# Two rows of output-norm gates: summed over partitions by square turns and memory instead of products with ones

## The chip, the cores and the metric

The kernel runs on one core of one Trainium2 chip. The metric is the device time of one execution in microseconds (us). Three runs of the kernel before took 1633.28, 1633.6 and 1634.9 us; their median, 1633.6 us, is the time that the prediction starts from. Engines are called TensorE (PE, and PEld for its weight loads), VectorE (DVE), ScalarE (ACT), GpSimd (POOL) and SyncE (SP).

## The reference, cut to what matters

One layer of a hybrid diffusion backbone works on 256 latent tokens of 2048 channels, with 256 context tokens. A vector `c` of 2048 numbers is turned into six vectors of 2048 by one matrix; two of them gate the outputs of the two sub-layers, after a norm:

```python
mod = jax.nn.silu(c) @ w_mod[l] + b_mod[l]
sh_m, sc_m, ga_m, sh_f, sc_f, ga_f = [m[:, None, :] for m in jnp.split(mod, N_MOD, axis=-1)]
...
x = x + ga_m * rms_norm(y, norm_post_mix[l])
h2 = modulate(rms_norm(x, norm_pre_mlp[l]), sh_f, sc_f)
x = x + ga_f * rms_norm(sq_relu_mlp(h2, mlp_w1[l], mlp_w2[l]), norm_post_mlp[l])
```

`rms_norm(y, g)` divides a token by its root mean square and multiplies by `g`. The gate and the norm's weight do not depend on the token, so the kernel folds them into one row, `gain_row = ga * norm_post`, of 2048 numbers for each sub-layer. Everything is float32, all tolerances included, so the large products run as three products of a high and a low part.

## The kernel before, in words

Weights come as a stream of tiles of 128x1024 float32 (512 KB each), fetched by SP into five `raw` buffers (line 86). For each tile ScalarE makes the high part (`whi`, line 124) and VectorE the low part (`wlo`, line 127), up to four tiles ahead of TensorE (`AHEAD`), which has four buffers of each. TensorE's products all go through line 188. In the second half of the program a step uses one tile in 12 matmuls of 512 columns (`tokens`, line 280): 4 accumulators (2 token blocks by 2 column blocks) by 3 terms. The last three tiles of a group are used together, accumulator by accumulator. Then the accumulators are evacuated, and the next group begins. The groups come in this order: `who` (2 groups of 8 tiles), `wpw` (2 of 8), `wo` (2 of 16), and then four times `up(q)` (2 of 16) and `down(q)` (2 of 16).

Small work is put between these steps by hand. A generator is pushed on a queue, and `pump(us)` (line 161) after each step advances up to three of them, in order, until their announced cost in us has used up a credit (1.3 or 1.4 us per step). A `yield None` ends a generator's turn until the next pump. `finish` runs a generator to its end.

The gate vectors are computed on VectorE. The 64 tiles of `wm1` are threaded into the weight stream, and `gemv` (line 1290) multiplies a tile by one number per partition and adds it to `gacc`, a page of 128x1024. After 16 tiles the 128 partial sums of each of 1024 columns lie in 128 partitions. There are four such halves: `gain_row(acc, i, h)` (line 1337), with `i` the sub-layer and `h` the half, is put at the head of the queue for each. The halves of `i = 0` end inside `wpw` and `wo` and are read in `wo`'s evacuation (`gained`, line 914), the first half from the end of the first group on, the second at the end of the second. Those of `i = 1` end around `down(1)` and in `up(3)` and are read at the very end (`gained2`, line 1034).

`gain_row` before: GpSimd loads the bias row (4 KB, line 1341) and the norm's weight, copied to all 128 partitions (512 KB, line 1342). VectorE adds the bias to partition 0 (line 1346). `split` (line 240) parts `gacc` into a high and a low half, on ScalarE and VectorE, 512 columns at a time. After three or four pumps TensorE multiplies them by a 128x128 matrix of ones (line 1360), four matmuls of 512 columns, which leaves the sum over partitions in every partition; VectorE multiplies by the weight into `gain_row` (line 1362). The flag `room`, set by `tokens`, holds the halves of `i = 1` until a step at which PSUM banks are free.

All buffers are handed out by a scheduler: 30 pages of 128x1024 (`page`), 8 PSUM banks, small tags. GpSimd's queue is in order and also carries the loads of `x` again (`xr`, line 894, four of 512 KB, issued in the program during `wo`'s first group, in time as soon as their pages are free) and `swapped` (lines 1284 and 1287), which turns the MLP's hidden blocks by a write to memory and four reads.

Of the kernel before, what the change touches and what calls it, by code (L numbers as in the profile page):

```python
# [8 lines left out]
F32 = mybir.dt.float32  # L9
F32R = mybir.dt.float32r  # L10
I32 = mybir.dt.int32
U8 = mybir.dt.uint8
AF = mybir.ActivationFunctionType
ALU = mybir.AluOpType

P = 128
T = 256
D = 2048
KT = D // P
DH = 1024  # L20
# [6 lines left out]
TW = 1024  # L27
# [110 lines left out]
class Kernel:  # L138
    def __init__(self, ctx, tc, a, out):
        self.tc = tc  # L140
        self.nc = tc.nc
        self.a = a
        self.out = out
        self.wp = ctx.enter_context(tc.tile_pool(name="wp", bufs=1))
        self.pg = ctx.enter_context(tc.tile_pool(name="pg", bufs=1))
        self.sp = ctx.enter_context(tc.tile_pool(name="sp", bufs=1))
        self.cp = ctx.enter_context(tc.tile_pool(name="cp", bufs=1))
        self.dr = ctx.enter_context(tc.tile_pool(name="dr", bufs=1, space=bass.MemoryType.DRAM))
        self.ps = ctx.enter_context(tc.tile_pool(name="ps", bufs=1, space=bass.MemoryType.PSUM))
        self.bg = collections.deque()  # L150
        self.his, self.los = [], []
        self.credit = 0.0
        self.queued = None
        self.room = True


    def push(self, gen):
# [119 lines left out]
            evac(b0, accs)  # L277
            self.pump(us)

    def tokens(self, x, evac, us, end=False, nk=KT, groups=2, pairs=False, pre=None, halves=False, begin=None, turnwise=False, keep=False):  # L280

# [11 lines left out]
        ahead = nk // 2 if turnwise else 0  # L295
        begun = []
        for g in range(groups if ahead else 0):
            self.room = not keep
            begun.append(banks(g))
            for k in range(ahead):  # L300
                if pre is not None:
                    pre(g, k)
                w = self.stream.next(AHEAD)
                for tb, j in order:
                    begun[g][1](w, k, tb, j)
                self.pump(us)
        for g in range(groups):
            last = end and g == groups - 1
            n = nk - (END if last else LAST)
            self.room = not keep  # L310
            accs, part = begun[g] if ahead else banks(g)
            for k in range(ahead, n):
                self.room = not keep or not ahead and 4 <= k < 7
                if pre is not None:
                    pre(g, k)
                w = self.stream.next(AHEAD)
                for tb, j in order:
                    part(w, k, tb, j)
                self.pump(us)
# [66 lines left out]
    def run(self):  # L386
        nc, a = self.nc, self.a
# [1 line left out]
        nc.sync.dma_start(pack, a["pack"])  # L389
        self.v = {n: pack[:, o:o + w] for n, (o, w) in _OFF.items()}  # L390
        v = self.v
        self.ones = self.cp.tile([P, P], F32, name="ones")
        nc.vector.memset(self.ones, 1.0)
        self.ones_r = self.cp.tile([P, P], F32R, name="ones_r")
        nc.scalar.copy(out=self.ones_r, in_=self.ones)
        self.grow, self.grow_gen = {}, {}
        self.mean = self.cp.tile([P, P], F32, name="mean")
        nc.vector.memset(self.mean, 1.0 / DH)
        self.eps = self.cp.tile([P, 1], F32, name="eps")
        nc.vector.memset(self.eps, EPS)  # L400
        self.vp = []
# [616 lines left out]
        def up(q):  # L1018
# [8 lines left out]
                if (tb, c % 2) == (1, 1):  # L1027
                    turns.setdefault(q, []).append(self.push(self.turn_hidden(hid, q, list(self.hidden))))
            self.hidden = [None, None]
            self.tokens(h2x, ev, 1.4, groups=2 if q else 1, keep=True)  # L1030
            self.finish(turns[q][0])

        def gained2(yp, tb, c, s=slice(0, 512)):
# [2 lines left out]
        def down(q):  # L1036
# [52 lines left out]
                        nc.vector.scalar_tensor_tensor(x1[:, s], self.cut(yp, tb, i)[:, s], r, x1[:, s], op0=ALU.mult, op1=ALU.add)  # L1089
                        nc.sync.dma_start(o[:, s], x1[:, s])  # L1090
            yp = self.pages(4, F32, "gained") if q == 3 else None
            self.tokens(lambda k: (self.at(uh_, k), self.at(ul_, k)), ev, 1.4, end=q == 3, halves=q == 3, pre=pre, turnwise=True, keep=True)

        for q in range(4):
            up(q)
# [241 lines left out]
    def gain_row(self, acc, i, h):  # L1337

        nc = self.nc
        g, b = self.page(F32, "gain")[:, :TW], self.page(F32, "bias")[0:1, :TW]  # L1340
        nc.gpsimd.dma_start(b, self.a["bgain"][2 * i + h:2 * i + h + 1, :])
        nc.gpsimd.dma_start(g, self.a["gain"][2 * i + h:2 * i + h + 1, :].partition_broadcast(P))
        yield None
        while not self.room:
            yield None
        nc.vector.tensor_tensor(acc[0:1, :], acc[0:1, :], b, op=ALU.add)
        parts = []
        for j in range(2):
            parts.append([self.sp.tile([P, 512], F32R, name="gpart", tag="t2", bufs=5) for i in range(2)])
            self.split(acc[:, j * 512:(j + 1) * 512], *parts[j])  # L1350
            yield 1.2
        for _ in range(3 if i else 4):
            yield None
        row = self.grow[i, h] = self.page(F32, "gain_row")[:, :TW]

        banks = [self.bank() for _ in range(8 if i else 2)]
        for j in range(2):
            ps = banks[j]
            for n, w in enumerate(parts[j]):
                nc.tensor.matmul(ps, self.ones_r, w, start=(n == 0), stop=(n == 1))  # L1360
            s = slice(j * 512, (j + 1) * 512)
            nc.vector.tensor_tensor(row[:, s], ps, g[:, s], op=ALU.mult)
            yield 0.6

    def values(self, ch, hx, tiles, begun=None):

# [327 lines left out]
```

## Time and profile before

| what | value |
|---|---|
| three runs | 1633.28, 1633.6, 1634.9 us |
| median | 1633.6 us |
| span of the profiled execution, first to last instruction | 1632.6 us |
| PE busy | 1615.6 us (99%) |
| PEld, DVE, ACT, POOL busy | 1337.5, 1162.2, 784.3, 52.0 us |
| granted TensorE clock, mean | 0.999 |
| DMA | 391.22 MB, mean 240 GB/s |

The profiled execution has no time of its own beside its span; the median lies 1.0 us above the span. A profile row names line, engine, operation, tiles (`out<-in`) and shape, then how often, busy us and mean ns, and last how long the engine had stood idle and what ended that. Rows of a timeline begin with the start in us from the span's start and the duration; neighbours of one kind are merged (x4). A matmul's duration contains its way through the array, so matmuls overlap, and what one costs is the distance between starts.

### The profile page before, as it was taken

The numbers are of one execution on the slowest core, as the hardware profiler recorded it, in microseconds if no ns is written. First come the engines' busy times: TensorE is split into PE (matmuls) and PEld (weight loads), VectorE is DVE, ScalarE is ACT, GpSimd is POOL, SyncE is SP. The second block draws the span as 40 slices with busy tenths as digits, with TensorE's granted clock in tenths as the row PEclk, the third lists the DMA queues.
The fourth block names the chain that finished last, engine by engine and source line by source line (L and its number), as shares of the span: only waits on it lengthen the run. The fifth ranks groups of instructions, "written<-read, shape, count | busy, mean of one in ns | idle before, by whom it ended". The sixth has DMA issues, their size and how long they took to land.

```text
span 1632.6 us, 21510 instructions
## 1 busy us (share of the span) xinstructions
PE 1615.6 (99%) x7939; PEld 1337.5 (82%) x7939; DVE 1162.2 (71%) x1686; ACT 784.3 (48%) x1094; POOL 52.0 (3%) x98
## 2 busy tenths in 40 slices
PE   7999999999999999999999999999999999999998
PEld 5668888888888888888888888888888888888887
DVE  5786887778868889977887676545665656665556
ACT  6553444434554444654446665444553455435543
POOL 0000000000000000000000001000110011001000
PEclk9999999999999999999999999999999999999999
DMA  9997954444566566787887478867887688677763
GB/s 377 402 379 281 324 175 151 149 152 135 194 202 219 182 192 205 236 279 267 320 302 254 142 259 256 287 197 235 289 283 227 217 255 284 231 240 241 232 217 114
DMA packets 109145, 391.22 MB, mean 240 GB/s; under 512 B 12912, under 2 KB 13680, under 8 KB 109040
## 3 DMA queue, kind: packets, MB, share of 16 engines
q1 hardware_dynamic: 102096, 368.60, 66.4%
q0 software_dynamic: 6656, 20.99, 4.3%
q8 instruction: 62, 1.02, 0.3%
q14 instruction: 43, 0.35, 0.1%
q10 hardware_dynamic: 288, 0.26, 0.0%
HBM read 379.32 MB, written 10.49 MB: 239 GB/s over the span
## 4 chain that ended last, share of the span: by engine, by line
PE 94%; DVE 2%; DMA 1%; issue 1%; ACT 1%; SPq 0%; ACTq 0%; DVEq 0%
PE bank L188 82%; PE bank L255 5%; PE bank L257 3%; PE bank L1465 2%; DVE wlo L127 1%; DMA x<-ctx 1%; ACT whi L124 0%; DMA raw<-who 0%; PE bank L1496 0%; PE bank L1507 0%; PE bank L1505 0%; DMA raw<-wpw 0%; DVE gacc L1301 0%; SPq L526 0%; PE bank L1360 0%
## 5 line engine op out<-in xcount | busy, mean ns | idle before, releaser
L127 DVE TENSOR_TENSOR wlo<-raw,whi 128x1024 fp32r<-128x1024 f32 x488 | 593.0, 1222 | 321.2 <-ACT whi L124 315.1
L124 ACT ACTIVATE whi<-raw 128x1024 fp32r<-128x1024 f32 x488 | 512.9, 1059 | 605.2 <-PE bank L188 388.5
L188 PE MATMUL bank<-whi,h 128*128 128x512 f32 x2160 | 674.1, 390 | 2.0 <-DVE h L673 1.2
L188 PEld LDWEIGHTS bank<-whi,h 128*128 128x128 f32 x2160 | 405.1, 188 | 88.0 <-DVE h L673 2.1
L188 PE MATMUL bank<-wlo,h 128*128 128x512 f32 x1080 | 420.7, 390 | 1.3 <-DVE wlo L127 1.3
L188 PEld LDWEIGHTS bank<-wlo,h 128*128 128x128 f32 x1080 | 202.8, 188 | 44.9 <-DVE wlo L127 3.5
L188 PE MATMUL bank<-whi,hidh 128*128 128x512 f32 x503 | 195.0, 388 | 0.0
L188 PE MATMUL bank<-wlo,hidh 128*128 128x512 f32 x503 | 195.0, 388 | 0.0
L188 PE MATMUL bank<-whi,hidl 128*128 128x512 f32 x503 | 195.0, 388 | 0.0
L188 PE MATMUL bank<-h,whi 128*128 128x512 f32 x512 | 166.2, 405 | 0.0
L188 PEld LDWEIGHTS bank<-whi,hidl 128*128 128x128 f32 x503 | 94.4, 188 | 19.5
L188 PEld LDWEIGHTS bank<-wlo,hidh 128*128 128x128 f32 x503 | 94.4, 188 | 19.3
L188 PEld LDWEIGHTS bank<-whi,hidh 128*128 128x128 f32 x503 | 94.4, 188 | 19.3
L188 PEld LDWEIGHTS bank<-h,whi 128*128 128x128 f32 x512 | 91.3, 189 | 20.6 <-issue 6.2
L188 PE MATMUL bank<-h,wlo 128*128 128x512 f32 x256 | 100.0, 391 | 0.0
L255 PE MATMUL bank<-h,whi 128*128 128x512 f32 x384 | 97.8, 396 | 0.0
L255 PEld LDWEIGHTS bank<-h,whi 128*128 128x128 f32 x384 | 69.0, 189 | 12.4
L1314 DVE SCALAR_TENSOR_TENSOR raw<-raw,silu_row 128x1024 f32<-128x1024 f32 x64 | 76.6, 1219 | 0.4 <-DMA raw<-wmt 0.3
L1301 DVE SCALAR_TENSOR_TENSOR gacc<-raw,silu_c,gacc 128x1024 f32<-128x1024 f32 x60 | 76.7, 1278 | 0.0
L188 PEld LDWEIGHTS bank<-h,wlo 128*128 128x128 f32 x256 | 48.1, 188 | 10.2
L257 PEld LDWEIGHTS bank<-h,wlo 128*128 128x128 f32 x384 | 52.4, 190 | 3.9
L257 PE MATMUL bank<-h,wlo 128*128 128x256 f32 x384 | 53.5, 282 | 0.0
(246 smaller groups left out, 1374.5 us busy)
## 6 DMA issues: line engine op xcount, KB each, us to landing
raw<-w SPq DMA_DIRECT2D x256, 512.0 KB, 4.8
raw<-wi SPq DMA_DIRECT2D x172, 512.0 KB, 4.5
raw<-wmt SPq DMA_DIRECT2D x64, 512.0 KB, 4.3
raw<-wm SPq DMA_DIRECT2D x64, 512.0 KB, 4.8
rawpage<-wm SPq DMA_DIRECT2D x42, 512.0 KB, 9.7
raw<-wo SPq DMA_DIRECT2D x32, 512.0 KB, 4.8
raw<-who SPq DMA_DIRECT2D x16, 512.0 KB, 5.1
raw<-wpw SPq DMA_DIRECT2D x16, 512.0 KB, 5.6
```

What stands on the lines that cost most here:

```text
L124: kn.his.append(nc.scalar.activation(out=hi, in_=raw, func=AF.Copy))
L127: kn.los.append(nc.vector.tensor_tensor(lo, raw, hi.bitcast(F32), op=ALU.subtract))
L188: ins = fn(*args, **kw)
L255: nc.tensor.matmul(bank, w[0][:, cut(i)], x(k)[2], start=(k == 0), stop=False)
L257: nc.tensor.matmul(bank[:, T:], w[1][:, cut(i)], x(k)[0], start=False, stop=(k == nk - 1))
L1301: nc.vector.scalar_tensor_tensor(acc, raw, s, acc, op0=ALU.mult, op1=ALU.add)
L1314: nc.vector.scalar_tensor_tensor(raw, raw, 1.0, self.srow, op0=ALU.mult, op1=ALU.mult, accum_out=self.dot[:, 32 * j + b:32 * j + b + 1])
L1465: nc.tensor.matmul(ps[:, b * P:(b + 1) * P], w, r, start=True, stop=True)
```

## The change

`gain_row` no longer uses TensorE or ScalarE. VectorE turns `gacc` in square blocks of 32x32 (`flip`), so that columns stand in partitions, and sums along the free dimension over the 32 rows of each block. That leaves, for each group of 32 partitions, 32 partial sums by 32 columns in `two` (128x32). GpSimd writes `two` to memory (`there`, 16 KB) and reads it back with the four groups side by side in 32 partitions (`back`). After five pumps VectorE adds the four (`whole`), turns the 32x32 result, adds the bias and multiplies by the weight; GpSimd writes that to memory as a row of 1024 (`line`, 4 KB) and reads it into all partitions (`row`, 512 KB). Bias and weight come as two 32x32 tiles (4 KB each). The ones in float32 go, the matrix of ones in float32r (still used by `warm`) is made from another constant, and `room` and `keep` go.

```diff
-        self.room = True
...
-    def tokens(self, x, evac, us, end=False, nk=KT, groups=2, pairs=False, pre=None, halves=False, begin=None, turnwise=False, keep=False):
+    def tokens(self, x, evac, us, end=False, nk=KT, groups=2, pairs=False, pre=None, halves=False, begin=None, turnwise=False):
...
-                self.room = not keep or not ahead and 4 <= k < 7
...
-        self.ones = self.cp.tile([P, P], F32, name="ones")
-        nc.vector.memset(self.ones, 1.0)
-        self.ones_r = self.cp.tile([P, P], F32R, name="ones_r")
-        nc.scalar.copy(out=self.ones_r, in_=self.ones)
...
+        self.ones_r = self.cp.tile([P, P], F32R, name="ones_r")
+        nc.scalar.activation(out=self.ones_r, in_=self.mean, func=AF.Copy, scale=float(DH))
...
     def gain_row(self, acc, i, h):
 
         nc = self.nc
-        g, b = self.page(F32, "gain")[:, :TW], self.page(F32, "bias")[0:1, :TW]
-        nc.gpsimd.dma_start(b, self.a["bgain"][2 * i + h:2 * i + h + 1, :])
-        nc.gpsimd.dma_start(g, self.a["gain"][2 * i + h:2 * i + h + 1, :].partition_broadcast(P))
-        yield None
-        while not self.room:
+        r = 2 * i + h
+        two = self.cp.tile([P, 32], F32, name="gsum", tag="gsum", bufs=1)
+        bg = self.cp.tile([32, 64], F32, name="gbias", tag="gbias", bufs=1)
+        for n, nm in enumerate(("bgain", "gain")):
+            nc.gpsimd.dma_start(bg[:, 32 * n:32 * n + 32], self.a[nm][r:r + 1, :].rearrange("o (n i) -> (o n) i", i=32))
+        flip = self.page(F32, "flip")[:, :TW]
+        for j in range(2):
+            s = slice(j * 512, (j + 1) * 512)
+            nc.vector.transpose(out=flip[:, s], in_=acc[:, s])
+            yield 0.7
+        for j in range(2):
+            s = slice(j * 512, (j + 1) * 512)
+            nc.vector.tensor_reduce(two[:, 16 * j:16 * j + 16], flip[:, s].rearrange("p (n j) -> p n j", j=32), axis=mybir.AxisListType.X, op=ALU.add)
+            yield 0.7
+        there = self.dr.tile([P, 32], F32, name="gsums", tag="gsums", bufs=2)
+        nc.gpsimd.dma_start(there, two[:, 0:32])
+        back = self.cp.tile([32, 4 * 32], F32, name="gback", tag="gback", bufs=1)
+        nc.gpsimd.dma_start(back.rearrange("i (b n) -> i b n", b=4), there.rearrange("(b i) n -> i b n", b=4))
+        for _ in range(5):
             yield None
-        nc.vector.tensor_tensor(acc[0:1, :], acc[0:1, :], b, op=ALU.add)
-        parts = []
-        for j in range(2):
-            parts.append([self.sp.tile([P, 512], F32R, name="gpart", tag="t2", bufs=5) for i in range(2)])
-            self.split(acc[:, j * 512:(j + 1) * 512], *parts[j])
-            yield 1.2
-        for _ in range(3 if i else 4):
+        whole = self.cp.tile([32, 64], F32, name="gwhole", tag="gwhole", bufs=1)
+        nc.vector.tensor_reduce(whole[:, 0:32], back.rearrange("i (b n) -> i n b", b=4), axis=mybir.AxisListType.X, op=ALU.add)
+        nc.vector.transpose(out=whole[:, 32:64], in_=whole[:, 0:32])
+        nc.vector.tensor_tensor(whole[:, 32:64], whole[:, 32:64], bg[:, 0:32], op=ALU.add)
+        nc.vector.tensor_tensor(whole[:, 32:64], whole[:, 32:64], bg[:, 32:64], op=ALU.mult)
+        yield 0.6
+        line = self.dr.tile([1, TW], F32, name="gline", tag="gline", bufs=2)
+        nc.gpsimd.dma_start(line.rearrange("o (n i) -> (o n) i", i=32), whole[:, 32:64])
+        row = self.grow[i, h] = self.page(F32, "gain_row")[:, :TW]
+        nc.gpsimd.dma_start(row, line.partition_broadcast(P))
+        for _ in range(5):
             yield None
-        row = self.grow[i, h] = self.page(F32, "gain_row")[:, :TW]
-
-        banks = [self.bank() for _ in range(8 if i else 2)]
-        for j in range(2):
-            ps = banks[j]
-            for n, w in enumerate(parts[j]):
-                nc.tensor.matmul(ps, self.ones_r, w, start=(n == 0), stop=(n == 1))
-            s = slice(j * 512, (j + 1) * 512)
-            nc.vector.tensor_tensor(row[:, s], ps, g[:, s], op=ALU.mult)
-            yield 0.6
```

## Rows read from the trace of the kernel before

**Rows 1.** The page: busy time by engine, the chain that ended last, one group.
```profile
PE 1615.6 (99%) x7939; PEld 1337.5 (82%) x7939; DVE 1162.2 (71%) x1686; ACT 784.3 (48%) x1094; POOL 52.0 (3%) x98
...
PE 94%; DVE 2%; DMA 1%; issue 1%; ACT 1%; SPq 0%; ACTq 0%; DVEq 0%
...
L127 DVE TENSOR_TENSOR wlo<-raw,whi 128x1024 fp32r<-128x1024 f32 x488 | 593.0, 1222 | 321.2 <-ACT whi L124 315.1
```

**Rows 2.** Waits, all engines: waiter <- awaited, us in total, times, longest.
```profile
ACT whi L124 <- PE bank L188: 388.5, 226, 5.7
```

**Rows 3.** Waits of TensorE alone, the same columns.
```profile
PE bank L188 <- DVE wlo L127: 1.3, 3, 0.9
```

**Rows 4.** Timeline of TensorE at the first half's products, 804 to 807 us.
```profile
805.25 1.09 PE L1360 MATMUL bank<-gpart,ones_r 128*128 128x512 f32 x4
806.18 0.39 PE L188 MATMUL bank<-whi,h 128*128 128x512 f32 x1
806.41 0.39 PE L188 MATMUL bank<-wlo,h 128*128 128x512 f32 x1
```

**Rows 5.** By tile: VectorE's operations that go, with count and ns min/median/max.
```profile
L240 DVE TENSOR_TENSOR gpart<-gacc,gpart x8: 678/682/693, 792.6 to 1506.0; 128x512 fp32r<-128x512 f32 x8
...
L1362 DVE TENSOR_TENSOR gain_row<-bank,gain x8: 677/680/693, 809.3 to 1514.9; 128x512 f32<-128x512 f32 x8
...
L1346 DVE TENSOR_TENSOR gacc<-gacc,bias x4: 1205/1206/1206, 788.8 to 1502.4; 1x1024 f32<-1x1024 f32 x4
```

**Rows 6.** Groups of VectorE by line and shape, nearest to what is added.
```profile
L1250 DVE STREAM_TRANSPOSE turned<-rsq 128x512 f32<-128x512 f32 x32 | 22.7, 709 | 26.1 <-ACT rsq L1025 25.7 <-ACT rsq L1240 0.4
...
L1569 DVE TENSOR_REDUCE lnred<-lnsq 128x256 f32<-128x1024 f32 x2 | 4.0, 2005 | 0.0
...
L429 DVE TENSOR_TENSOR lb_mx<-lb_e 128x16 f32<-128x16 f32 x1 | 0.2, 174 | 1.1 <-ACT lb_e L428 1.1
```

**Rows 7.** Timeline of GpSimd, 1140 to 1210 us: writes to memory, reads behind them.
```profile
1141.18 0.56 POOL L1284 DMA_DIRECT2D there<-turned  x1 [112.54 <-DVE turned L1250]
1144.39 2.18 POOL L1287 DMA_DIRECT2D back<-there  x4 [2.65 <-DMA there<-turned]
...
1157.79 2.18 POOL L1287 DMA_DIRECT2D back<-there  x4 [9.60 <-ACT whi L124]
...
1202.62 0.51 POOL L1341 DMA_DIRECT2D bias<-bgain  x1
```

**Rows 8.** By line: GpSimd's bias loads of 4 KB, with issue to landing.
```profile
L1341 POOL DMA_DIRECT2D bias<-bgain x4: 499/508/625, 708.4 to 1377.8; - x4
...
DMA to landing us min/median/max: 3.2/5.8/8.1
```

**Rows 9.** Weight rows of 512 KB to all partitions, the same view.
```profile
L1342 POOL DMA_DIRECT2D gain<-gain x4: 547/575/575, 710.1 to 1378.3; - x4
...
DMA to landing us min/median/max: 5.7/8.0/10.2
```

**Rows 10.** Timeline of GpSimd, 783 to 815 us: the loads of `xr`, first and third.
```profile
783.44 0.54 POOL L894 DMA_DIRECT2D xr<-x  x1 [72.78 <-PE bank L188]
...
795.30 0.53 POOL L894 DMA_DIRECT2D xr<-x  x1 [4.49 <-DVE gpart L240]
```

**Rows 11.** Windows: busy us by engine (x), PEclk, DMA share, GB/s.
```profile
790.00:800.00 10.00, 9.83 (x43) 7.73 (x42) 8.43 (x9) 6.03 (x7) 1.06 (x2) 1.00 0.99 366
810.00:820.00 10.00, 10.00 (x54) 8.43 (x54) 9.06 (x10) 4.91 (x6) 1.05 (x2) 1.00 0.98 356
```

**Rows 12.** Timeline of TensorE, 797 to 799 us.
```profile
798.53 0.50 PE L188 MATMUL bank<-wlo,h 128*128 128x512 f32 x1 [0.17 <-DVE wlo L127]
```

**Rows 13.** Timeline of VectorE, 874 to 914 us: the second half's last sum, its reader.
```profile
876.54 1.28 DVE L1301 SCALAR_TENSOR_TENSOR gacc<-raw,silu_c,gacc 128x1024 f32<-128x1024 f32 x1
...
908.32 0.69 DVE L914 TENSOR_TENSOR y<-bank,gain_row 128x512 f32<-128x512 f32 x1 [1.18 <-ACT junk L364]
912.39 0.16 DVE L377 TENSOR_REDUCE rtok<-ssq 128x1 f32<-128x4 f32 x1 [3.39 <-ACT junk L364]
```

More of the change, by code (lines that the diff above doesn't have):

```diff
@@ L297, in tokens @@
         for g in range(groups if ahead else 0):
-            self.room = not keep
             begun.append(banks(g))
@@ L309, in tokens @@
             n = nk - (END if last else LAST)
-            self.room = not keep
             accs, part = begun[g] if ahead else banks(g)
             for k in range(ahead, n):
-                self.room = not keep or not ahead and 4 <= k < 7
                 if pre is not None:
@@ L1029, in up @@
             self.hidden = [None, None]
-            self.tokens(h2x, ev, 1.4, groups=2 if q else 1, keep=True)
+            self.tokens(h2x, ev, 1.4, groups=2 if q else 1)
             self.finish(turns[q][0])
@@ L1091, in down @@
             yp = self.pages(4, F32, "gained") if q == 3 else None
-            self.tokens(lambda k: (self.at(uh_, k), self.at(ul_, k)), ev, 1.4, end=q == 3, halves=q == 3, pre=pre, turnwise=True, keep=True)
+            self.tokens(lambda k: (self.at(uh_, k), self.at(ul_, k)), ev, 1.4, end=q == 3, halves=q == 3, pre=pre, turnwise=True)
         for q in range(4):
```

## The prediction

> **What bounds the kernel now.** I read the page first: TensorE is busy for 1615.6 of 1632.6 us, and 94% of the chain that ended last is TensorE's own work [rows 1]. Busy time could hide matmuls that merely wait, so I read the waits next. ScalarE waits 226 times, 388.5 us in all, for TensorE to give back a weight buffer [rows 2], while TensorE waits for a low part only three times, 1.3 us in all [rows 3]. Weights are ready early, TensorE is late: a matmul more or less moves the end by its own length, unless it falls where TensorE waits anyway.
>
> What a matmul costs is the distance of starts, not the 0.39 us of its row: ordinary ones start 806.41 - 806.18 = 0.23 us apart. The four products with ones run from 805.25 to 806.18, 0.93 us [rows 4].
>
> How far the weights lead follows from this. A step is 12 x 0.23 = 2.8 us. When ScalarE has waited for a buffer, three ready tiles lie ahead of the one it now makes: 3 x 2.8 = 8.3 us. Making it takes VectorE 1.22 us [rows 1] and ScalarE no more before that, so the lead is some 8.3 - 2.4 = 5.9 us. VectorE may stand still that long in the plain steps without harm to TensorE; at the head of a group, and where the stream is late, for less.
>
> **The change, part by part.** *Removed on TensorE.* Sixteen products with ones, four per half, at 0.93 us per half: 4 x 0.93 = **3.7 us** off the path. Their weight loads overlap matmuls and cost nothing more. The low bound is nothing, if TensorE then waits for something else; the rows give no reason for more.
>
> *Removed and added on VectorE.* Removed per half: 1.21 (bias, on one partition, yet as long as a whole page) + 2 x 0.68 + 2 x 0.68 = 3.93 us [rows 5]. Added: two turns of 128x512 at 0.71 = 1.42 us; two sums of 128x512 to 128x16; four small operations at about 0.17 = 0.7 us [rows 6]. The trace has no such sum. Nearest are the sums of 128x1024, 2.005 us with strided reads [rows 6], half of that is 1.00; from below, an elementwise operation of the same size takes 0.68 us [rows 5]. I take 1.0, the same kind of operation. Added: 1.42 + 2.0 + 0.7 = 4.1 us (3.5 by the low end), against 3.93. The Trainium skill, "VectorE: DVE Perf Modes", Rules for kernel authors, speaks against the change: a sum along partitions isn't possible on VectorE and belongs on GpSimd, and a `tensor_reduce` is its slowest operation, at one element per cycle. By its figure, at 0.96 GHz, 512 elements take an estimated 0.53 us, and the half would come to 3.2 us instead of 4.1; no run here shows one yet. Either way VectorE's load hardly changes, the 5.9 us of lead cover it, and it counts nothing. ScalarE loses two operations per half and never bound the path.
>
> *The added waits.* Before, nothing on VectorE waited for data from memory here; now the first of the four small operations waits for `back`, and all of VectorE's later work is queued behind it, the low parts first, for which TensorE would wait. A write to memory and the start of the read behind it took 0.56 + 2.65 = 3.2 us alone, and 0.56 + 9.60 = 10.2 us when issued behind four other transfers [rows 7]. Two such legs are 6.4 to 20.4 us; the generator leaves five pumps, 13.8 us. I take 3.2 for each where GpSimd's queue is empty (three halves), so no wait. For the first half of `i = 1`, whose bias load at 1202.62 follows a `swapped` without a gap [rows 7], the far end is 20.4 - 13.8 = 6.6 us of VectorE standing still, against 5.9 of lead: 0 to 0.7 us, taken as 0.1, since only one transfer can be that far behind.
>
> *GpSimd's queue.* Six transfers per half instead of two, 24 for 8; at 0.5 to 0.6 us of issue [rows 8, 9] that is 9 us more on an engine busy for 52.0 [rows 1]. What counts is the order. For the first half, `there` waits for VectorE, `back` for `there`, `line` for the small operations, `row` for `line`; the four loads of `xr` are queued behind all that. They used to go out between 783 and about 805 us [rows 10]; now the small operations stand where the products stood, 805 [rows 4], and 0.7 for them and 3.2 for `line` put the loads at about 810. They are read in `wo`'s evacuation, tens of us later, so their lateness alone costs nothing. But the stretch they leave had a DMA share of 0.99 and TensorE waiting (0.17 us) for a low part [rows 11, 12]; the stretch they enter has 0.98 already [rows 11]. One is relieved, the other loaded: -0.2 and +0.3, bounds below. The granted clock is 1.00 in both [rows 11], the upper level (2.4 GHz), TensorE being busy before and after; no term for it.
>
> *The end of `wo`.* The second half's last sum is done at 877.8; with 3.4 us of turns and sums and a low part between, the sums are ready at about 882.5. Five pumps later, at 896 or before, come the small operations, 0.7; then `line` and `row`: alone 3.2 and 5.7 [rows 8, 9], so about 905.6. Its reader ran at 908.32, and VectorE then stood idle for 3.39 us [rows 13], so harm begins at about 911.7. Nothing is added here. The halves of `i = 1` are read at the very end, long after.
>
> *Pages, banks, start.* A page less and a few banks fewer per half only loosen the scheduler. The ones' memset goes from VectorE's first instructions, ahead of any data; nothing.
>
> The sum: -3.7 - 0.2 + 0.3 + 0.1 = **-3.5 us**, with -3.7 - 1.3 = -5.0 as the best end (all of TensorE's waits for low parts gone as well). Against the span, 1632.6 - 3.5 = 1629.1; the median lies 1.0 us above the span, and so the time is 1633.6 - 3.5 = 1630.1 us.
>
> **Rivals.** *The burst.* Four `xr` loads and `row` leave together at about 810 us, when the stream is just in time. For: the 0.98. Against: the stream has used the freed stretch to run ahead, up to five raw tiles. The four loads are 2.1 MB, 5.7 us at 366 GB/s [rows 11]; if half the lead is there, 3.0 us, TensorE loses 2.7: 1632.8 us. Nothing to all of 5.7 is the bound.
>
> *The row comes too late* (the slower side). Place: the end of `wo`, where VectorE evacuates in order and TensorE waits for it to begin `up(0)`. Legs at the far ends, 10.2 + 10.2 from 882.5, make `back` land at 902.9; 0.7, 8.1 and 10.2 more [rows 7 to 9] make 921.9: 10.2 us after the 911.7 at which harm begins, so 1630.1 + 10.2 = 1640.3. It decides once `line` and `row` together take over 15.0 us (911.7 - 896.7), against 8.9 alone. For: every leg here is a round through memory. Against: the far ends of the rows stand behind `swapped`, and there is none before 970 us. The Trainium skill, "DMA: Bandwidth & Descriptors", Anatomy of one DMA, puts a GpSimd transfer at about 2.0 us plus its bytes over 436 GB/s; by that `line` and `row` are an estimated 5.2 us, and this rival still further off. The 3.2 for 4 KB [rows 8] lies above it.
>
> *It doesn't shorten TensorE's path.* If the weights are what the end waits for, the freed slots turn into waits for `wlo`: 1633.6. For: the first half lies in such a stretch [rows 12]. Against: 1.3 us of such waits in the whole run [rows 3].
>
> **How the numbers follow.** Forecast 0.60, burst 0.24, no shortening 0.07, late row 0.09. About 0.2% (3.3 us) can be told from no change: faster is below 1630.3, slower above 1636.9. The forecast's own range, 1628.6 to 1630.6, lies mostly below 1630.3: 0.52 of 0.60, and 0.01 of the burst with almost no loss; faster 0.53. The late row gives slower 0.09, same is the rest, 0.38. The range goes from 1628.6, the best end, over the burst to the kernel before with its spread, 1634.2; the late row and a burst at its full price are left out.
>
> **What would show it.** Right: no TensorE matmul on ones outside `warm`; start-to-start 0.23 us through the places of the four halves; VectorE waiting for `back` under 1 us each; `row` landing before 908 us; PE busy lower by about 3.5 us. Wrong: TensorE waits for `wlo` above 1.3 us, between 810 and 835 us for the burst; VectorE at line 914 ended by a DMA near 908 us for the late row.

## The result, and the profile after

The changed kernel takes 1630.69 us (median of 19 runs, 1628.80 to 1631.62), the kernel before 1633.88 us beside it (19 runs, 1632.21 to 1634.90): a ratio of 0.998 with a 95% interval of 0.9974 to 0.9987, or 3.2 us less. Forecast were 1630.1 us and 3.5 us less. The kernel is faster for certain (the whole interval lies below 1), but by just under the 3.3 us that the prediction set as its bound for "faster": by that bound this is "no different", to which it gave 0.38 against 0.53 for "faster". The interval lies on both sides of the bound.

The page of the changed kernel: span, busy time by engine, shares of the chain that ended last.

```profile
span 1629.3 us, 21503 instructions
...
PE 1612.0 (99%) x7923; PEld 1333.7 (82%) x7923; DVE 1159.7 (71%) x1697; ACT 779.7 (48%) x1086; POOL 60.6 (4%) x114
...
PE 85%; issue 5%; DMA 5%; DVE 3%; ACT 1%; POOL 0%; SPq 0%; ACTq 0%; DVEq 0%; POOLq 0%
```

Against [rows 1] TensorE has 16 instructions and 3.6 us less, and that is nearly all that the time shows. GpSimd is busy 8.6 us longer (9 forecast), VectorE 2.5 us shorter. The chain now has 85% of TensorE instead of 94%, and this is no loss of 9%: where TensorE stops for a moment, the chain turns off to what it waited for and follows that back, through tens of us in which TensorE was busy as well. Two such detours are shown below.

Waits of TensorE for a low part, in the same view as [rows 3], where they were 1.3 us in three waits:

```profile
PE bank L187 <- DVE wlo L127: 2.1, 3, 0.9
```

They were expected to shrink; they grew, which the prediction had named as a sign of being wrong. One of the three, 0.9 us at 33.91, lies in the start and stands in every profile of this study (0.8 to 0.9); the other two were 0.35 us and are now 1.2. The timeline of TensorE has them, and a third stop that this view doesn't list (start, duration, last the idle time and its releaser; a row `x2` holds two matmuls 0.23 us apart, an ordinary distance is 0.23):

```profile
796.69 0.62 PE L187 MATMUL bank<-whi,h 128*128 128x512 f32 x2
798.03 0.50 PE L187 MATMUL bank<-wlo,h 128*128 128x512 f32 x1 [0.72 <-DVE wlo L127]
798.37 0.63 PE L187 MATMUL bank<-whi,h 128*128 128x512 f32 x2
...
904.34 0.39 PE L187 MATMUL bank<-whi,zh 128*128 128x512 f32 x1
905.22 0.50 PE L187 MATMUL bank<-wlo,zh 128*128 128x512 f32 x1 [0.49 <-DVE wlo L127]
...
1214.69 0.39 PE L187 MATMUL bank<-whi,hidh 128*128 128x512 f32 x1
1215.15 0.50 PE L187 MATMUL bank<-wlo,hidh 128*128 128x512 f32 x1
```

A stop costs the distances of starts over 0.23. At 798.03 it is 798.03 - 796.69 - 2 x 0.23 = 0.88, and the next distance of 0.34 adds 0.11: 1.0 us. At 905.22 it is 0.65, and 0.10 by the next distance: 0.75. At 1215.15 it is 0.23 and 0.11: 0.34. (The third has no idle time in its row: a matmul's duration covers it. Only the distance of starts shows it.) The kernel before lost by the same reckoning 0.45 us at 798.53 [rows 12] and 0.45 us at 754.48; the latter stop is gone. Why is not shown: with nothing changed but the products taken out it is gone as well, and in another profile below it stands with 0.9 us.

For the sum, the path has two rows that both kernels have: the first `pack,o` matmul of the readout, where the second part of the program begins, and the last diagonal matmuls. First the kernel before, then the changed one, on TensorE's timeline:

```profile
658.33 1.12 PE L1533 MATMUL bank<-pack,o 128*128 128x128 f32 x4 [0.19 <-DVE o L1528]
...
1625.94 1.13 PE L1083 MATMUL bank<-gained,diag 128*128 128x256 f32 x4 [0.28 <-ACT diag L1081]
```

```profile
657.82 1.11 PE L1535 MATMUL bank<-pack,o 128*128 128x128 f32 x4 [0.19 <-DVE o L1530]
...
1622.93 1.13 PE L1077 MATMUL bank<-gained,diag 128*128 128x256 f32 x4 [0.28 <-ACT diag L1075]
```

Between the two lie 967.61 us before and 965.11 after. I call this **the path**; it leaves out the start, which differs by 2 us between profiles (the first of the two rows lies between 656.93 and 659.07 in the profiles of this study) with TensorE's waits for `x` and the context. So this execution gained 2.5 us on the path, and the parts give that: -3.7 (products) + (1.0 - 0.45) - 0.45 + 0.75 + 0.34 = -2.5 us. The other 0.8 of the 3.3 us between the two spans lies ahead of and behind the path (0.5 and 0.3), which the change hardly touches and which differs from profile to profile; the medians are the measure. All path differences rest on one profile of the kernel before. The changed kernel's profiled run took 1631.12 us, 1.8 above its span; by the same distance, an estimate, that of before took 1634.4, half a us above its median. So half a us of a path difference may be that execution's own.

What the new operations cost on VectorE, by line (count, ns min/median/max, first and last start):

```profile
L1342 DVE STREAM_TRANSPOSE flip<-gacc x8: 669/699/711, 786.0 to 1472.4; 128x512 f32<-128x512 f32 x8
...
L1346 DVE TENSOR_REDUCE gsum<-flip x8: 643/673/678, 787.2 to 1473.6; 128x16 f32<-128x512 f32 x8
...
L1355 DVE TENSOR_REDUCE gwhole<-gback x4: 358/376/381, 808.8 to 1492.5; 32x32 f32<-32x128 f32 x4
```

A sum of 128x512 takes 0.67 us, not the 1.00 taken. The small sum takes 0.38 and its three companions 0.17 to 0.20 each, 0.92 together instead of 0.7. A half is thus 1.40 + 1.35 + 0.92 = 3.7 us of VectorE against 3.93 before [rows 5].

VectorE's wait for the trip through memory (waiter <- awaited: us in total, times, longest):

```profile
DVE gwhole L1355 <- DMA gback<-gsums: 9.8, 2, 7.0
```

Two of the four halves wait, 9.8 us together; forecast were less than 1 us each, but for one.

### The profile page after: what moved, and what is told of

Its sections match the earlier page's. It is cut to its first block, busy times and chain, and to the rows that moved or that the text cites. A ratio compares the mean times of both kernels' runs of the same rounds, so it can differ in the third digit from the quotient of the medians.

```text
span 1629.3 us, 21503 instructions
## 1 busy us (share of the span) xinstructions
PE 1612.0 (99%) x7923; PEld 1333.7 (82%) x7923; DVE 1159.7 (71%) x1697; ACT 779.7 (48%) x1086; POOL 60.6 (4%) x114
## 3 DMA queue, kind: packets, MB, share of 16 engines
q8 instruction: 62, 1.02, 0.3%
## 4 chain that ended last, share of the span: by engine, by line
PE 85%; issue 5%; DMA 5%; DVE 3%; ACT 1%; POOL 0%; SPq 0%; ACTq 0%; DVEq 0%; POOLq 0%
PE bank L187 73%; PE bank L254 5%; PE bank L256 3%; PE bank L1467 2%; DMA raw<-wi 1%; DVE wlo L127 1%; ACT whi L124 1%; DMA rawpage<-wms 1%; DMA gback<-gsums 1%; DMA x<-ctx 1%; DMA raw<-wpw 1%; DMA raw<-w 1%; PE bank L1498 0%; DMA raw<-wo 0%; PE bank L1509 0%
## 5 line engine op out<-in xcount | busy, mean ns | idle before, releaser
L254 PEld LDWEIGHTS bank<-h,whi 128*128 128x128 f32 x384 | 69.0, 189 | 12.4
```

Of the source, the lines that this page charges most:

```text
L254: nc.tensor.matmul(bank, w[0][:, cut(i)], x(k)[2], start=(k == 0), stop=False)
```

## The experiments

The theory after these readings: each product is on the path at 0.23 us, the 3.7 us are all gained, and 1.2 us are given back since VectorE's new operations and its wait for `gback` let weights come late. The rivals: the products were partly hidden, and the gain comes from what else moved (the weight rows, the loads of `xr`); or the late weights come from full DMA engines, not from VectorE.

Each kernel ran on the same chip as runs of the kernel before, in three groups; in this order: medians of before 1633.80 us (27 runs: after again, no products, idle products, no pumps), 1633.67 (30 runs: more pumps, spread, both, late row) and 1633.38 (23 runs: no weight loads, both again, after a third time). "Path" is that of the one profiled execution.

| run | median us (runs) | ratio to before | path us |
|---|---|---|---|
| before | 1633.88 (19) | 1 | 967.61 |
| after | 1630.69 (19) | 0.998, 0.9974 to 0.9987 | 965.11 |
| after again | 1631.15 (11) | 0.9981, 0.9972 to 0.9990 | 965.38 |
| after a third time | 1630.40 (11) | 0.9982, 0.9973 to 0.9991 | 963.58 |
| no products | 1633.06 (11) | 0.9991, 0.9983 to 1.0000 | 966.03 |
| no weight loads | 1630.16 (11) | 0.9982, 0.9973 to 0.9991 | 965.27 |
| idle products | 1645.43 (4) | 1.0072, 1.0059 to 1.0086 | 979.94 |
| no pumps | 1636.04 (10) | 1.0013, 1.0004 to 1.0022 | 972.25 |
| more pumps | 1629.87 (11) | 0.9977, 0.9968 to 0.9986 | 965.67 |
| spread | 1630.33 (11) | 0.9980, 0.9971 to 0.9989 | 963.94 |
| both | 1629.24 (9) | 0.9974, 0.9964 to 0.9983 | 962.87 |
| both again | 1628.65 (7) | 0.9973, 0.9962 to 0.9984 | 962.92 |
| late row | 1636.97 (9) | 1.0019, 1.0009 to 1.0028 | 971.73 |

**The changed kernel again**, twice, to see which stops recur.

> The changed kernel once more, to see what of its profile recurs. Theory (the three waits of TensorE for a low part are made by the change): they stand again at about 797, 904 and 1215 us, with about 2 us of TensorE lost, VectorE waits again for the read-back in the second and third half, and the time is about 3.2 us below the kernel before. Rival (they are accidents of one profile): they stand elsewhere or are gone.

> The changed kernel a third time, for the comparison with both edits. Theory: the stops at 797 and 904 us stand again, 1630.5 to 1631.5 us.

Measured: 2.65 and 2.98 us less than before. The stop near 797 comes back in the first (0.8 us by distances) and not in the third, where the same matmuls run on at 0.23; there a stop of 0.3 us stands at 820.7. The stop near 904 comes back in both, 1.6 and 0.3 us, and the one at 1215 in neither. So these stops do not come in every execution: weights arrive there with little or no lead. The waits of VectorE behind two of them do recur: 9.6 and 7.3 us in two waits each.

**What a product costs.** The changed kernel with 16 unread products with ones per half put back:

```diff
         for _ in range(5):
             yield None
+        ps = self.bank()
+        for _ in range(16):
+            nc.tensor.matmul(ps.rearrange("p (o t) -> p o t", o=4), self.ones_r, self.ones_r.rearrange("p (o t) -> p o t", o=1).broadcast_to([P, 4, P]), start=True, stop=True)
```

> The changed kernel with sixteen matmuls of 512 columns per half that nobody reads, four times what was taken out. Theory (each costs its distance of starts, 0.227 to 0.233 us): 64 of them add 14.5 to 14.9 us to the changed kernel, 1645.4 us, a ratio of 1.007 to the kernel before. Rival (TensorE has idle slots there): less than 10 us.

Measured: 1645.43 us, 14.3 us above the changed kernel of the same group, and 14.6 to 14.8 us on the path (against that group's profile and the first), for 64 products: 0.22 to 0.23 us each. TensorE's timeline at the first half's sixteen (the row merges them; the next matmul starts 807.52 - 803.84 = 3.68 us later, 0.23 each):

```profile
803.84 3.84 PE L1356 MATMUL bank<-ones_r 128*128 128x512 f32 x16
807.52 0.39 PE L187 MATMUL bank<-whi,h 128*128 128x512 f32 x1
```

A product is on the path at its full distance of starts, at these four places. The rival by which the freed slots turn into waits is worth nothing there, as far as adding goes.

**Only the products taken out**, everything else of the kernel before left.

```diff
-        banks = [self.bank() for _ in range(8 if i else 2)]
         for j in range(2):
-            ps = banks[j]
-            for n, w in enumerate(parts[j]):
-                nc.tensor.matmul(ps, self.ones_r, w, start=(n == 0), stop=(n == 1))
             s = slice(j * 512, (j + 1) * 512)
-            nc.vector.tensor_tensor(row[:, s], ps, g[:, s], op=ALU.mult)
+            nc.vector.tensor_tensor(row[:, s], parts[j][1].bitcast(F32), g[:, s], op=ALU.mult)
```

> The kernel before without the sixteen products: what is left out is the sum over partitions, the rows are made from one part of the partial sums. Theory (the products lie on TensorE's path at full price): 3.7 us below the kernel before, 1630.2 us, a ratio of 0.9977, and TensorE's waits for low parts as before, 1.3 us. Rival (the freed slots turn into waits): no difference, and more than 4 us of waits for low parts.

Measured: 1633.06 us, 0.7 us less than before, not 3.7. The profile shows where the rest stays (TensorE's waits for low parts, then the timelines of GpSimd, ScalarE and TensorE):

```profile
PE bank L188 <- DVE wlo L127: 3.1, 3, 2.0
```

```profile
811.89 0.55 POOL L1342 DMA_DIRECT2D gain<-gain  x1
...
819.58 1.06 ACT L124 ACTIVATE whi<-raw 128x1024 fp32r<-128x1024 f32 x1 [3.63 <-DMA raw<-wpw]
...
824.92 0.50 PE L188 MATMUL bank<-wlo,h 128*128 128x512 f32 x1 [1.99 <-DVE wlo L127]
```

TensorE, earlier by a half's products, meets tiles that are not there yet: 2.0 us of idle time that the kernel before did not have. ScalarE waited 3.63 us for a tile of `wpw`, and just ahead of that GpSimd had sent for the second half's weight row, 512 KB. Here the rival "it doesn't shorten TensorE's path" did hold, for more than half of the gain. How much varies: the 11 runs lie between 1631.03 and 1634.37 us, and the profiled one took 1633.51.

**The same, without the two weight rows of `i = 0`** (VectorE multiplies two parts of the partial sums with each other instead; that line and the products are left out here).

```diff
-        g, b = self.page(F32, "gain")[:, :TW], self.page(F32, "bias")[0:1, :TW]
+        g, b = self.page(F32, "gain")[:, :TW] if i else None, self.page(F32, "bias")[0:1, :TW]
...
-        nc.gpsimd.dma_start(g, self.a["gain"][2 * i + h:2 * i + h + 1, :].partition_broadcast(P))
+        if i:
+            nc.gpsimd.dma_start(g, self.a["gain"][2 * i + h:2 * i + h + 1, :].partition_broadcast(P))
```

> The kernel before without the products and also without the two 512 KB loads of the norm's weight in the first sub-layer (left out: the sum over partitions everywhere, the weight in two rows). The kernel without the products alone stopped for 2.2 us at 822.5 us. Theory (the slots freed on TensorE are lost again there because the weight stream is late, and the 512 KB that move from 811.9 us on make it late): the stop falls under 0.5 us and the time is 3.5 us or more below the kernel before, 1630.3 us or less. Rival (the stop has another cause, four loads of x before it or VectorE): it stays near 2 us, and the time near 1633.

Measured: 1630.16 us, 3.2 us less than before. TensorE's timeline has in place of the stop of 2.0 us:

```profile
822.05 0.50 PE L188 MATMUL bank<-wlo,h 128*128 128x512 f32 x1
```

By distances that is 0.24 us, and the DMA engines' share between 810 and 820 is 0.81 instead of 0.92. By the medians 2.5 us of the gain have come back, by the paths of the two profiles 0.8 (this profile has stops of 0.9 us near 753 and 1.2 us near 797, where the kernel before has one of 0.45 each). So the gain needs both: fewer matmuls, and less traffic across the stream behind 805. What traffic is not separated: without the weight rows the last load of `xr`, which waits for a page, went early as well, so that all four are out by 794.98 us, where no products sends it at 805.65. The changed kernel has neither there: it loads 4 KB, its 512 KB rows go at 817 and at 896, and the `xr` loads at 818.

**Without the five pumps** ahead of the small operations, in all halves:

```diff
-        for _ in range(5):
+        for _ in range(0):
             yield None
         whole = self.cp.tile([32, 64], F32, name="gwhole", tag="gwhole", bufs=1)
```

> The changed kernel with no pump between the read-back and its first use, so that VectorE stands still for both trips through memory in all four halves: 7.0, 9.8, 11.6 and 6.1 us by the landings in the changed kernel's profile, 34.5 in all. Theory (VectorE's standing still costs TensorE what goes beyond the lead of ready weights, 5.9 us in plain steps, about 2 at the head of a group and where the stream is late): 5 + 7 + 4.6 + 0.2 us lost on TensorE against 2 now, so 13 to 17 us above the changed kernel, about 1646 us. Rival (the lead covers it everywhere): within 2 us of the changed kernel.

Measured: 1636.04 us, 4.9 above the changed kernel of the same group, 7.1 on the path. That is the right direction and a third of the size. VectorE's wait, TensorE's stop with what followed, and a window with its clock (busy us by engine, granted clock, share of the DMA engines, GB/s):

```profile
DVE gwhole L1355 <- DMA gback<-gsums: 18.3, 4, 7.4
```

```profile
798.82 0.50 PE L187 MATMUL bank<-wlo,h 128*128 128x512 f32 x1 [3.07 <-DVE wlo L127]
...
800.27 0.71 PE L187 MATMUL bank<-wlo,h 128*128 128x512 f32 x1 [0.49 <-DVE wlo L127]
800.78 1.05 PE L187 MATMUL bank<-whi,h 128*128 128x512 f32 x2
801.63 0.63 PE L187 MATMUL bank<-wlo,h 128*128 128x512 f32 x1
```

```profile
800.50:803.30 2.80, 2.80 (x7) 2.16 (x7) 2.73 (x4) 0.00 (x0) 0.52 (x2) 0.50 0.91 270
```

VectorE waits in all four halves, 18.3 us; TensorE loses by distances 5.7 us in the first half, 0.4 at 826, 2.1 around 909 and 0.7 at 1221. So about half of the waits is covered, and the first half, where the stream has no lead, bears most of the rest. The forecast was too high, in part because VectorE waited 18.3 us and not 34.5: it still had ready tiles to make before it came to `gback`. A part of the 5.7 is the clock: after the stop the granted clock is 0.50 (1.2 GHz) for a while (1.00 again from 804 to 808), and the nine distances from 800.27 on take 3.75 us instead of 2.0, 1.7 us more.

**More pumps**, where VectorE had waited: seven in the second half, nine elsewhere.

```diff
-        for _ in range(5):
+        for _ in range(7 if (i, h) == (0, 1) else 9):
             yield None
```

> The changed kernel with nine pumps instead of five between the read-back and its first use, seven in the second half, whose row is wanted soon. Theory (VectorE's wait for the read-back, 9.8 and 9.6 us in two profiles, lets the weights fall behind): the wait falls under 1 us, TensorE's stop at about 904 us (0.8 and 1.6 us lost) goes, the one at 797 stays, and the time is 0.8 to 1.6 us below the changed kernel. Rival (the 512 KB of the row, which now move at 896 to 903 us, hold up the weights): the stop stays, or comes some 3 us later.

Measured: 1629.87 us. VectorE no longer waits for `gback`, and the stops at 904 and 1215 are gone; that part of the theory stands. The median is 3.8 us below that of before, against 2.65 to 3.2 for the changed kernel. But the path of the profiled run, the longest of the 11 with 1632.05 us, is not shorter (965.67): the stop near 797 stays, with 0.8 us, and in the first half four pumps more move `gain_row` and the four loads of `xr` from 818 to 826, where they meet the first tiles of `wo`. GpSimd's and TensorE's timelines of this kernel:

```profile
826.85 2.15 POOL L888 DMA_DIRECT2D xr<-x  x4
...
840.79 0.49 PE L187 MATMUL bank<-whi,zh 128*128 128x512 f32 x1 [0.70 <-ACT whi L124]
842.04 0.50 PE L187 MATMUL bank<-wlo,zh 128*128 128x512 f32 x1 [0.76 <-DVE wlo L127]
```

The distances from 839 to 842 give 1.8 us. This is the burst of the prediction's first rival, at another place than it was looked for. That it comes from the loads, and not from the later pumps as such, is only argued from their time; with five pumps in the first half and nine only in those of `i = 1` (both, below) there is no such stop.

**The first half's four operations spread**, one per pump instead of four in a row:

```diff
-            yield 0.7
+            yield None if (i, h) == (0, 0) else 0.7
```

(in both loops)

> The changed kernel with the two turns and two sums of the first half one to a pump instead of four in a row. Theory (2.5 us of VectorE in a row hold back a low part, and with it a raw buffer and the next fetch): SyncE's gap before the fetch at 789.6 us shrinks from 4.1 to about 2 us, and TensorE's stop at 797 (0.8 to 1.0 us) falls to the 0.45 of the kernel before or below; 0.5 us of time. Rival (the stream is simply short of memory bandwidth there): the stop stays near 1 us.

Measured: 1630.33 us, a path of 963.94, and no stop at 797. SyncE's timeline, the fetches of weight tiles, in the changed kernel and then in this one:

```profile
785.47 0.33 SPq L86 DMA_DIRECT2D raw<-wm  x1
789.58 0.99 SPq L86 DMA_DIRECT2D raw<-wpw  x2
```

```profile
785.21 0.33 SPq L86 DMA_DIRECT2D raw<-wm  x1
787.53 0.99 SPq L86 DMA_DIRECT2D raw<-wpw  x2
```

In a row, the four operations hold up VectorE for 2.5 us (786.0 to 788.4); the low part and the gate product (`gacc`, line 1293) behind them free their `raw` buffers that much later, and SyncE sends for nothing for 4.1 us instead of 2.3. The chain of waits of the changed kernel, cut to that stretch, tells the same (start, us, what):

```profile
786.04 1.21 DVE flip L1342 x2
...
789.47 0.76 DVE gacc L1293
...
790.24 5.31 DMA raw<-wpw
...
798.03 2.11 PE bank L187 x8
```

The gap on SyncE is there in all three profiles of the changed kernel, the stop in two of them, and neither the 1.2 us between the paths 965.11 and 963.94 nor the 0.2 to 0.7 us by medians is more than runs and profiles of the changed kernel differ. What is shown is the late fetch, not a loss each time. How much the stop at 797 costs on the average of runs stays open; it is less than the medians can tell.

**Both**: spread in all halves but the second, seven pumps in the second half, five in the first, nine in those of `i = 1`.

```diff
-            yield 0.7
+            yield None if (i, h) != (0, 1) else 0.7
...
-        for _ in range(5):
+        for _ in range(7 if (i, h) == (0, 1) else 5 if i == 0 else 9):
```

> Both edits: the four operations one to a pump in all halves but the second, and nine pumps in the halves of the MLP, seven in the second half. Theory: both stops gone or under 0.5 us, 1.3 to 2 us below the changed kernel, about 1629 us, a ratio of 0.997 to the kernel before, the best of all. Rival: no different from the changed kernel.

> The kernel with both edits once more, beside the changed kernel on the same chip. Theory: no stop for a low part above 0.5 us at 797, 904 or 1215 us, about 1629 us, 1 to 2 us below the changed kernel. Rival: the two are the same to within 0.5 us.

Measured: 1629.24 and 1628.65 us, 4.4 and 4.7 us less than before; paths of 962.87 and 962.92, 4.7 us less. The stops at 797, 904 and 1215 are gone, and TensorE's only wait for a low part is the 0.9 us in the start. The gain is then the 3.7 us of products and the two stops of 0.45 us that the kernel before had. VectorE's reader at the end of `wo` now waits a little for its row (1.5 and 2.0 us, and 2.5 in more pumps), and TensorE loses nothing by it:

```profile
908.19 0.69 DVE L908 TENSOR_TENSOR y<-bank,gain_row 128x512 f32<-128x512 f32 x1 [1.55 <-DMA gain_row<-gline]
```

This version beats the kernel before by 0.27% and the changed kernel of its group by 1.75 us (1630.40 to 1628.65); the ranges of their runs overlap by 0.2 us (1628.45 to 1629.64 against 1629.41 to 1632.17).

**The row made late on purpose**, for the rival that had the slower side: the second half's small operations behind forty pumps, so that they come when the generator is run to its end.

```diff
-        for _ in range(5):
+        for _ in range(40 if (i, h) == (0, 1) else 5):
```

> The changed kernel with the second half's last steps held back until its reader asks for them, so that the write of the row and its spreading, 1.6 and 7.0 us in the changed kernel, stand right in front of the reader at about 909 us. Theory (the late-row rival, as priced in the prediction): VectorE waits some 9 us there, all but 0.7 to 3.4 us of that is lost, 5.5 to 8.5 us, less the stop at 904 that goes: about 1636 us, slower than the kernel before. Rival (TensorE has enough to do until then): within 1 us of the changed kernel.

Measured: 1636.97 us, slower than before by 3.3 us; the path is 6.6 us longer than the changed kernel's. VectorE's wait, TensorE's stop, and the window behind it:

```profile
DVE y L908 <- DMA gain_row<-gline: 5.4, 1, 5.4
```

```profile
922.76 1.11 PE L187 MATMUL bank<-pack,y 128*128 128x128 f32 x4 [6.17 <-DVE y L958]
```

```profile
923.50:925.50 2.00, 2.00 (x7) 1.61 (x6) 0.52 (x2) 1.16 (x3) 0.00 (x0) 0.50 0.00 0
```

The mechanism is real: a row that VectorE awaits for 5.4 us at 911 to 917 stops TensorE for 6.2, since evacuations run in order and `up(0)` begins behind them. In the changed kernel it does not happen: its row has landed before VectorE asks for it.

## Why the prediction was right, and where its steps were not

*Sixteen products at 0.23 us, 3.7 us: right.* Idle products put back cost 0.23 us each, and the version without other losses gains 4.7, which is 3.7 plus the stops of before. The low end of the forecast's range, 5.0 us less with all waits gone, counted the 0.9 us in the start, which stayed; the best version reaches 4.7.

*The transfers that go or move: left without a price.* The step on GpSimd's queue counted six transfers for two and followed the loads of `xr`, but gave no price to the 512 KB row that no longer leaves at 812, nor to the `xr` load that no longer leaves at 805. The products alone gained 0.7 us by the medians, and without the rows (and with the load gone ahead) 3.2. The forecast needed this part and had it by luck: with those transfers where they were, most of the 3.7 us was lost again by the medians, as by the "no shortening" rival, put at 0.07.

*"The generator leaves five pumps, 13.8 us": mis-sized.* The pumps follow TensorE's steps in the program, but VectorE need not run at TensorE's pace. Where several ready tiles wait for it, as behind the new operations, it makes them in a row: four in the second half, three in the third. Its timeline in the third half (start, duration, last the idle time):

```profile
1199.71 1.24 DVE L1346 TENSOR_REDUCE gsum<-flip 128x16 f32<-128x512 f32 x2
1200.87 3.49 DVE L127 TENSOR_TENSOR wlo<-raw,whi 128x1024 fp32r<-128x1024 f32 x3
...
1213.37 0.38 DVE L1355 TENSOR_REDUCE gwhole<-gback 32x32 f32<-32x128 f32 x1 [7.05 <-DMA gback<-gsums]
```

From the end of the sums (1200.95) to the point where VectorE was ready for `gback` (1213.37 - 7.05 = 1206.32) there were 5.4 us, not 13.8; in the second half 7.4. The trip took 12.4 us in the third half, behind `swapped`, within the 6.4 to 20.4 that bounded it. So VectorE stood 7.05 us in the third half (6.6 forecast as the far end, for the wrong reason) and 2.8 us in the second, where none was forecast. The chain of waits of the second half, up to the stop at 905.22 (start, us, what):

```profile
886.72 5.83 DMA gback<-gsums
...
892.64 0.39 DVE gwhole L1355
...
894.75 1.22 DVE wpage L127
...
895.99 6.76 DMA raw<-wo
...
903.94 1.24 DVE wlo L127
```

VectorE waits for `gback`, its low parts come late (`wpage` is that of a tile kept in a page), so the next tile of `wo` is sent for late, and its low part is done at 905.18, when TensorE has run out.

*"The lead covers 5.9 us": right in the plain steps, too much where the stream is late.* The wait of 7.05 us in the third half cost TensorE 0.34 us (nothing in the two other profiles, with 6.6 and 5.3), that of 2.8 us in the second half, with the stream late and `wo` ending, 0.75 us: the smaller wait cost more, as the prediction's own proviso has it, which it then left without a price. It put 0.1 us in the sum for what came to 1.1. That seven pumps in the second half end both the wait and the stop at 904 (more pumps, both), while the spread first half leaves them, ties the stop to the wait, and so does the chain above. One part is not separated: the 512 KB row left at 896.13, beside that fetch, and may have lengthened its 6.76 us; with seven pumps it leaves at 900 to 903.

*"The stretch 790 to 800 is relieved, -0.2": wrong sign in this profile.* The `xr` loads did leave it, and the share of the DMA engines fell from 0.99 [rows 11] to 0.88. But the stop grew from 0.45 to 1.0 us. VectorE's four operations now stand in one row: the sum counted them as load, 4.1 against 3.93 us, and not as a block in which no buffer is freed. That the fetch behind them is late is shown; the stop followed in two profiles of three. The prediction read the full share ahead of the old stop as its cause. No run shows what caused that one; the new one came with emptier DMA engines, behind transfers that had not started.

*The burst, +0.3: no loss in this profile, 0.3 us in another (the stop at 820.7, whose cause is not shown).* The windows of the changed kernel, in the view of [rows 11]:

```profile
790.00:800.00 10.00, 9.28 (x42) 7.34 (x41) 8.12 (x9) 3.35 (x4) 0.56 (x1) 1.00 0.88 320
820.00:830.00 10.00, 10.00 (x46) 8.29 (x45) 9.50 (x13) 3.19 (x3) 0.07 (x1) 1.00 1.02 403
```

The loads of `xr` left at 817.93, not 810, because the row ahead of them in GpSimd's queue went at 817.37; 403 GB/s ran through 820 to 830 with TensorE busy throughout. The rival of 2.7 us is refuted here. In more pumps, with the loads nine us later, 1.8 us were lost, by them as far as their time tells.

*VectorE's sum at 1.00 us: too long, 0.67 measured.* It changed nothing, as forecast. The prediction's estimate by the Trainium skill, "VectorE: DVE Perf Modes", Rules for kernel authors, was 0.53, which counts one element per cycle and nothing else; the measured value lies nearer to it than to the 1.00. The Trainium skill's rule there, that a sum along partitions is not for VectorE, doesn't bind here: square turns and a trip through memory do it, and VectorE works 3.67 us per half instead of 3.93.

*The end of `wo`: right.* `gain_row` was sent for at 896.13 (GpSimd) and landed at 903.1, the reader ran at 909.49 without waiting; 905.6 and 911.7 were forecast for landing and harm. There `line` and `row` took 1.6 and 7.0 us (1.6 and up to 7.7 in the two other profiles), against the 15.0 together at which the rival begins. Rows that came 1.5 to 2.5 us late for VectorE cost TensorE nothing (both, more pumps), one of 5.4 us cost 6.2 (late row).

The sum as it came out in the profiled path: -3.7 + 0.55 (stretch 790 to 800) - 0.45 (754.48) + 0.75 + 0.34 = -2.5; over the three profiles -2.5, -2.2 and -4.0, mean -2.9; by medians -3.2, -2.65 and -2.98. The main term was right. The others missed in this profile by +0.75 (the stretch 790 to 800), +1.0 (the waits), -0.3 (the burst) and -0.45 (the stop at 754), together 1.0 us less gain than forecast. That the medians come as near as 0.3 to 0.9 us is luck in part: the relief without which most of the 3.7 us is lost was not in the sum.

## What to carry to other kernels

Where one engine is busy 99% of the time, a removed instruction is worth its distance of starts only if the inputs of the next one are there that much earlier: look at what else crosses the stream in the same 20 us, and price removed transfers as well as removed work. Count the distance between two program points on the clock of the engine that will wait, not of the engine that paces the program; here 13.8 us on one were 5.4 and 7.4 on the other. Small operations on an engine that recycles buffers are safer one per step: what has to be counted is not only the sum of their time but the longest stretch in which no buffer is freed. Four in a row sent a fetch 1.8 us later here.

## What was not expected of the hardware

After the stops of 3.07 and 6.17 us (no pumps, late row) the granted clock was 0.50, the lower of TensorE's two levels (1.2 of 2.4 GHz), and starts stood 0.43 us apart for about 3 us before it was 1.00 again; after the stop of 1.99 us (no products) the window 825 to 828 has 1.00 and 0.23. A long stop thus cost more than its length, 1.7 us more in the first case.

Small transfers are not all quick. In the changed kernel's profile, 16 KB written to memory landed after 1.7 to 6.8 us and were back after another 3.8 to 5.8; 4 KB written landed after 1.6 to 7.7 us. Around the two slowest writes the share of the DMA engines was 1.02 (1201 to 1209 us) and 0.98 (1496 to 1504), around the two quickest 0.44 (788.7 to 790.7) and 0.18 (893.9 to 896); the slow ones also stood behind transfers of `swapped` in GpSimd's queue, so which of the two delays them is not shown.
